# Mixer A of a two-layer backbone: GpSimd's subtraction reads the cumulated log-decays from the gates' tile, without VectorE's copy per head

## The chip, the cores and the metric

The kernel runs on one core of a Trainium2 chip. A core has five engines, each with its own queue of instructions, which it works off in order: TensorE (PE in the profile, with PEld for its weight loads), VectorE (DVE), ScalarE (ACT), GpSimd (POOL) and SyncE (SP), which here issues the transfers. They wait for one another through semaphores. The metric is the device time of one execution in microseconds, lower is better; for several runs the median is given.

## The reference

One inference step of a hybrid backbone with two layers, a width of 2048 and 640 tokens (128 context tokens, 512 latent tokens). The first layer has two mixers beside each other: gated-DeltaNet heads (mixer A) and windowed attention heads (mixer B). The second layer has gated linear attention and neighbourhood attention. Mixer A has 8 heads and works in chunks of 64 tokens, forwards and backwards. What matters here, for one head and one direction:

```python
gc = jnp.cumsum(g, -1)                                   # cumulated log-decays of a chunk
decay = jnp.exp(jnp.where(tri, gc[..., :, None] - gc[..., None, :], NEG))
lmat = jnp.where(strict, jnp.einsum('bhncd,bhnsd->bhncs', kb, k) * decay, 0.0)
attn = jnp.where(tri, jnp.einsum('bhncd,bhnsd->bhncs', q, k) * decay, 0.0)
```

The matrix of differences gc(c) - gc(s) is needed for each of the 10 chunks and the two directions; it enters both the triangular system `lmat`, which is then inverted, and the attention matrix `attn`.

## The kernel before

The weights are streamed from HBM in blocks of 128 x 512 (tile `w_st`). ScalarE rounds each block to a high part (`w_hi`, L1050) and VectorE subtracts this from the block for the low part (`w_lo`, L1052). TensorE multiplies the activations, split in the same way into `hh` and `hl`, in three products per block into PSUM tiles named `acc`. These products make up most of TensorE's work. All of them, and all small matmuls, go through one helper (L77).

Mixer A's heads run one after another through four stages, as generators: a convolution (`a_conv`), the preparation (`a_prep`), an inverse of the triangular matrices (`a_invert`, on GpSimd, with 60 small instructions and then one that transposes, L499), and the scan over the chunks (`a_scan`). Head h+1 is prepared while head h is inverted and scanned, and mixer B's heads and the weight products are laced in between. A planner in the kernel's own code chooses the order in which these generators issue: it keeps a clock that only matmuls advance and due times for each step. TensorE's order is fixed to that (`keep_in_program_order`). The orders of the other four queues are set by the framework, which sorts instructions by a simulated clock (`schedule_with_timeline_sim=True`) and puts in the semaphores. A tile with one buffer can only be written again when all readers of its former content are done; the framework makes the writer wait for that.

Before the heads, `a_gates` computes the gates of all heads once. The cumulated log-decays stand in the tile `g_gc` (128 partitions x 80 columns, ordered as direction o, chunk b, head h, so that one head's ten values lie 8 columns apart), and, transposed, in HBM (`gc_d`). `A["gc"]` is a view of `g_gc` with the axes o, b and h. In `a_prep`, for one head:

- SP issues two transfers that spread the head's rows of `gc_d` over 64 partitions each: tile `a_df`, 128 x 10 x 64, one buffer (L251).
- VectorE copies the head's ten columns of `g_gc` into `a_gcu`, 128 x 10, one buffer (L253).
- TensorE forms Gram matrices of the keys and the queries for their norms, VectorE reduces them (L270, L271), and a row of small VectorE instructions makes scale factors from them (L274 to L298).
- GpSimd subtracts `a_gcu`, each value repeated 64 times, from `a_df` in place (L301), and then adds a mask into `a_at` (L302).
- VectorE makes `a_M` from `a_df` (L309, L310), ScalarE takes exponentials, GpSimd scales `a_M` (L315).
- TensorE forms two more Gram products, each into a PSUM tile of the pool "gen", which has two buffers; VectorE multiplies them into `a_M` and `a_at` (L321), and the inverse starts with transfers of `a_M` to HBM and back into `i_S` (L482 to L489, GpSimd's first instruction is L491). Its results come back as `i_X` (L521), for the products `i_vps`.

The tiles of the pool "gen" are shared with the other small products, among them `ada_ps`, part of the modulation of later layers, which VectorE adds into `adv` (L1288). The scan's steps (L380 to L433) use PSUM tiles named `a_st`; VectorE's L410 and ScalarE's L412 both scale the same product, L427 updates the state. GpSimd's subtraction for head h+1 stands in GpSimd's queue right behind L315 of head h, ahead of the inverse of head h.

Of the kernel before, what the change touches and what calls it, by code (L numbers as in the profile page):

```python
# [8 lines left out]
F32 = mybir.dt.float32  # L9
# [3 lines left out]
ALU = mybir.AluOpType  # L13
# [76 lines left out]
def rsqrt(g, pool, x, n, tag, bufs=1):  # L90

    nc = g.nc
    y = pool.tile([128, n], F32, name=f"{tag}_y", tag=f"{tag}_y", bufs=bufs)[0:x.shape[0]]
    t = pool.tile([128, n], F32, name=f"{tag}_t", tag=f"{tag}_t")[0:x.shape[0]]
    yi = y.bitcast(I32)
    nc.vector.tensor_scalar(out=yi, in0=x.bitcast(I32), scalar1=1, scalar2=None, op0=ALU.logical_shift_right)
    nc.vector.tensor_scalar(out=yi, in0=yi, scalar1=-1.0, scalar2=float(0x5F3759DF), op0=ALU.mult, op1=ALU.add)
    for _ in range(3):
        nc.vector.tensor_mul(t, y, y)
        nc.vector.scalar_tensor_tensor(out=t, in0=t, scalar=-0.5, in1=x, op0=ALU.mult, op1=ALU.mult)  # L100
        nc.vector.scalar_tensor_tensor(out=y, in0=t, scalar=1.5, in1=y, op0=ALU.add, op1=ALU.mult)
    return y
# [137 lines left out]
def a_prep(g, h, qT, kT):  # L240

    nc, c, A = g.nc, g.c, g.A
    W, P1 = g.paw, g.pa1
    U = [128, 2, 5]
    hs = lambda t: t[:, :, :, h]
    bc = lambda t, n: t.unsqueeze(3).to_broadcast([128, 2, 5, n])


    df = W.tile([128, 10, 64], F32, name="a_df", bufs=1)
    for lo, hi in HALVES:  # L250
        nc.sync.dma_start(df[lo:hi], g.gcd[:, :, h, lo:hi].rearrange("o b s -> (o b) s").unsqueeze(0).to_broadcast([64, 10, 64]))  # L251
    gcu = W.tile([128, 10], F32, name="a_gcu")
    nc.vector.tensor_copy(gcu.rearrange("p (o b) -> p o b", o=2), hs(A["gc"]))  # L253
    b10 = lambda t: t.unsqueeze(2).to_broadcast([128, 10, 64])
    at = g.pe.tile([128, 2, 5, 64], F32, name="a_at", tag="a_at", bufs=2)
    M = P1.tile([128, 2, 5, 64], F32, name="a_M")
    def gram(x):

        ps = g.psg.tile([128, 5, 64], F32, name="a_gram", tag="gen")
        for b in range(5):  # L260
            for hf in range(2):
                cc = b * 128 + hf * 64
                g.mm(ps[hf * 64:hf * 64 + 64, b], lhsT=x[0][:, cc:cc + 64], rhs=x[1][:, cc:cc + 64], start=True, stop=True,
                     tile_position=(0, hf * 64))
        return ps

    ss = W.tile([128, 2, 5], F32, name="a_ss")
    for i, (x, sq) in enumerate(((kT, M), (qT, at))):
        ps = gram((x, x))
        nc.vector.tensor_tensor(out=sq[:, 0], in0=ps, in1=c["i64"].unsqueeze(1).to_broadcast([128, 5, 64]), op=ALU.mult)  # L270
        nc.vector.tensor_reduce(out=ss[:, i], in_=sq[:, 0], op=ALU.add, axis=mybir.AxisListType.X)  # L271
        yield
    sse = W.tile([128, 2, 5], F32, name="a_sse")
    nc.vector.tensor_scalar_add(sse, ss, 4 * EPS)  # L274
    rr = rsqrt(g, W, sse.rearrange("p a b -> p (a b)"), 10, "a_rr", bufs=2)
    rk, rq = rr[:, 0:5], rr[:, 5:10]
    rkb = rk.unsqueeze(1).to_broadcast(U)

    sm = lambda n: W.tile(U, F32, name=n, bufs=2)
    fm = c["fm"].rearrange("p (o b) -> p o b", o=2)  # L280
    bm = c["bm"].rearrange("p (o b) -> p o b", o=2)
    a = W.tile(U, F32, name="a_a")
    rk2 = W.tile([128, 5], F32, name="a_rk2")
    nc.vector.tensor_mul(rk2, rk, rk)
    nc.vector.tensor_mul(a, hs(A["beta"]), rk2.unsqueeze(1).to_broadcast(U))
    p2 = sm("a_p2")
    nc.vector.tensor_mul(p2, bm, sse[:, 0].unsqueeze(1).to_broadcast(U))
    nc.vector.tensor_add(p2, p2, hs(A["bfm"]))
    nc.vector.scalar_tensor_tensor(out=p2, in0=p2, scalar=0.5, in1=rkb, op0=ALU.mult, op1=ALU.mult)
    p1 = sm("a_p1")  # L290
    nc.vector.tensor_mul(p1, a, fm)
    nc.vector.tensor_add(p1, p1, bm)
    nc.vector.scalar_tensor_tensor(out=p1, in0=p1, scalar=-1.0, in1=hs(A["egc"]), op0=ALU.mult, op1=ALU.mult)
    c1 = sm("a_c1")
    nc.vector.tensor_mul(c1, a, bm)
    nc.vector.tensor_add(c1, c1, fm)
    c2 = sm("a_c2")
    nc.vector.tensor_mul(c2, c1, hs(A["dl"]))  # L298


    nc.gpsimd.tensor_tensor(out=df, in0=df, in1=b10(gcu), op=ALU.subtract)  # L301
    nc.gpsimd.tensor_tensor(out=at, in0=df.rearrange("p (o b) s -> p o b s", o=2),  # L302
                            in1=c["maskA"].rearrange("p (o s) -> p o s", o=2).unsqueeze(2).to_broadcast([128, 2, 5, 64]),
                            op=ALU.add)
    Mu = M.rearrange("p o b s -> p (o b) s")
    for o, (lo, hi) in enumerate(HALVES):
        f, b = slice(o * 5, o * 5 + 5), slice(5 - o * 5, 10 - o * 5)
        ms = c["maskS"][lo:hi].unsqueeze(1).to_broadcast([64, 5, 64])
        nc.vector.scalar_tensor_tensor(out=Mu[lo:hi, f], in0=df[lo:hi, f], scalar=-1.0, in1=ms, op0=ALU.mult, op1=ALU.add)  # L309
        nc.vector.tensor_tensor(out=Mu[lo:hi, b], in0=df[lo:hi, b], in1=ms, op=ALU.add)  # L310
    nc.scalar.activation(M, M, AF.Exp)
    nc.scalar.activation(at, at, AF.Exp)
    an = W.tile([128, 10], F32, name="a_an")
    nc.vector.tensor_scalar_mul(an, a.rearrange("p o b -> p (o b)"), -1.0)
    nc.gpsimd.tensor_tensor(out=Mu, in0=Mu, in1=b10(an), op=ALU.mult)  # L315


    yield LAT["gram"]
    for dst, x in ((M, kT), (at, qT)):
        ps = gram((kT, x))  # L320
        nc.vector.tensor_tensor(out=dst, in0=ps.unsqueeze(1).to_broadcast([128, 2, 5, 64]),  # L321
                                in1=dst, op=ALU.mult)
        if dst is M:
            inv = a_invert(g, M)
        yield
    return dict(h=h, qT=qT, kT=kT, inv=inv, at=at, p1=p1, p2=p2, c1=c1, c2=c2, rq=rq)
# [149 lines left out]
def a_invert(g, M):  # L476

    nc, W, P1 = g.nc, g.paw, g.pa1
    d1 = g.pd.tile([6, 10, 32, 32], F32, name="inv_in", tag="inv_in")
    for q in range(4):  # L480
        sub = q % 2
        nc.sync.dma_start(d1[q].rearrange("u i j -> i u j"),  # L482
                          M[q * 32:q * 32 + 32].rearrange("p o b s -> p (o b) s")[:, :, sub * 32:sub * 32 + 32])
        if sub == 1:
            nc.sync.dma_start(d1[4 + q // 2].rearrange("u i j -> i u j"),
                              M[q * 32:q * 32 + 32].rearrange("p o b s -> p (o b) s")[:, :, 0:32])
    SY = P1.tile([128, 1024], F32, name="i_S").rearrange("p (i j) -> p i j", i=32)
    S, Yt = SY[0:40], SY[64:104]
    nc.sync.dma_start(S, d1[0:4].rearrange("q u i j -> (q u) i j"))  # L489
    E = nc.gpsimd  # L490
    E.memset(S.rearrange("p i j -> p (i j)")[:, 0:1024:33], 1.0)  # L491
    for j in range(1, 31):
        n = 31 - j
        t = P1.tile([40, 240], F32, name="i_tmp", bufs=2)[:, 0:n * j].rearrange("p (a b) -> p a b", a=n)
        E.tensor_tensor(out=t, in0=S[:, j + 1:, j].unsqueeze(2).to_broadcast([40, n, j]),  # L495
                        in1=S[:, j, 0:j].unsqueeze(1).to_broadcast([40, n, j]), op=ALU.mult)
        E.tensor_tensor(out=S[:, j + 1:, 0:j], in0=S[:, j + 1:, 0:j], in1=t, op=ALU.add)  # L497
    Y = S
    E.tensor_tensor(out=Yt, in0=Y.rearrange("p i j -> p j i"), in1=g.c["ones"][0:40, 0:32].unsqueeze(1).to_broadcast([40, 32, 32]),  # L499
                    op=ALU.mult)  # L500
    d2 = g.pd.tile([2, 4, 10, 32, 32], F32, name="inv_out", tag="inv_out")
    nc.sync.dma_start(d2[0].rearrange("q u i j -> (q u) i j"), Y)
    nc.sync.dma_start(d2[1].rearrange("q u i j -> (q u) i j"), Yt)
    return d1, d2
# [1482 lines left out]
```

## Time and profile before

| | us |
|---|---|
| median of 3 runs | 2742.47 |
| lowest and highest | 2734.63 and 2742.68 |
| the profiled execution, its own time | 2739.52 |
| its span in the profile | 2737.7 |

The profile is of one execution. A row of a group or a timeline names line, engine, operation and tiles (written <- read); in a timeline the first number is the start in us from the span's start, the second the time it took, and in square brackets stands the idle time of the engine just before it with what ended it. In a table of waits stand the waiting instruction, whom it waited for, and the total in us, the number of times and the longest. The head's stage of mixer A lies between 180 and about 1110 us of the span. "Idle before" of an engine that is not the bottleneck costs nothing.

### The profile page before, as it was taken

The page shows a single profiled execution, that of the slowest core. Times are in us where ns is not written, and L with a number is a line of the kernel's source. Part 1 is how long each engine was busy: PE and PEld are TensorE (multiplying, and loading weights), DVE is VectorE, ACT ScalarE, POOL GpSimd, SP SyncE. Part 2 cuts the span into 40 slices and gives each one's busy share as a digit, 9 for nine tenths or more (in the row PEclk, how much of TensorE's full clock was granted, in tenths as well). Part 3 has the DMA queues.
Part 4 walks back from the last instruction along what each step waited for, and adds up shares of the span by engine and source line. Part 5 has one row for each costly group of instructions (what it writes and reads, how often), then busy time and mean ns, then how long its engine had stood idle before and what let it go on. Part 6 is the DMA issues. An engine that isn't in the chain of part 4 may idle for free. (4 is left out here: it accounts for less than half of the span.)

```text
span 2737.7 us, 54643 instructions
## 1 busy us (share of the span) xinstructions
PE 2606.5 (95%) x21303; PEld 2438.9 (89%) x21303; DVE 1542.8 (56%) x3606; ACT 954.4 (35%) x2150; POOL 703.9 (26%) x894
## 2 busy tenths in 40 slices
PE   6989999999999999999999899999999999999997
PEld 5778787988878897798999899999999999998996
DVE  5766546555556564447886745545553645545225
ACT  3232343423433343434224533343333334243222
POOL 2426604152342542001223330022001301221123
PEclk9989999999999999999999999999999999999998
DMA  9922333243333424236663423222232322325334
GB/s 336 314 88 83 115 94 107 87 120 107 91 116 100 137 68 121 82 110 221 193 203 119 129 70 105 95 86 86 88 115 80 95 88 90 101 68 182 94 101 135
DMA packets 264706, 329.85 MB, mean 120 GB/s; under 512 B 76013, under 2 KB 148925, under 8 KB 264447
## 3 DMA queue, kind: packets, MB, share of 16 engines
q1 hardware_dynamic: 264447, 326.35, 38.0%
q8 instruction: 168, 2.75, 0.4%
q14 instruction: 91, 0.75, 0.1%
HBM read 294.95 MB, written 28.68 MB: 118 GB/s over the span
## 5 line engine op out<-in xcount | busy, mean ns | idle before, releaser
L77 PE MATMUL acc<-hh,w_hi 128*128 128x320 f32 (+1 forms) x4544 | 1447.4, 320 | 15.7 <-ACT w_hi L1050 3.4
L77 PE MATMUL acc<-hl,w_hi 128*128 128x320 f32 (+1 forms) x4544 | 1416.1, 312 | 7.9 <-DVE hl L1230 7.7
L77 PE MATMUL acc<-hh,w_lo 128*128 128x320 f32 x4480 | 1394.0, 311 | 5.0 <-DVE w_lo L1052 5.0
L77 PEld LDWEIGHTS acc<-hh,w_hi 128*128 128x128 f32 (+1 forms) x4544 | 856.7, 189 | 56.7 <-issue 33.8
L77 PEld LDWEIGHTS acc<-hl,w_hi 128*128 128x128 f32 (+1 forms) x4544 | 857.5, 189 | 13.4 <-DVE hl L1230 11.5
L77 PEld LDWEIGHTS acc<-hh,w_lo 128*128 128x128 f32 x4480 | 846.8, 189 | 7.1 <-DVE w_lo L1052 6.3
L1052 DVE TENSOR_TENSOR w_lo<-w_st,w_hi 128x512 fp32r<-128x512 f32 x561 | 443.7, 792 | 583.3 <-ACT w_hi L1050 580.6
L1050 ACT CAST w_hi<-w_st 128x512 fp32r<-128x512 f32 (+1 forms) x604 | 365.0, 605 | 920.3 <-PE acc L77 790.9
L1321 DVE SCALAR_TENSOR_TENSOR vec<-vec,cond 128x256 f32<-128x256 f32 (+1 forms) x360 | 210.8, 629 | 24.0 <-DMA vec<-w_ada 22.3
L497 POOL TENSOR_TENSOR i_S<-i_S,i_tmp 40x30 f32<-40x30 f32 (+14 forms) x240 | 140.8, 587 | 18.7
L495 POOL TENSOR_TENSOR i_tmp<-i_S 40x30 f32<-40x30 f32 (+14 forms) x240 | 133.5, 556 | 18.0
L1464 POOL TENSOR_TENSOR n_acc<-n_acc,n_sq 128x640 f32<-128x640 f32 (+1 forms) x30 | 45.9, 1530 | 297.9 <-ACT n_sq L1463 297.9
L77 PE MATMUL ada_ps<-adv,cond 128*32 128x128 f32 x2048 | 93.6, 291 | 24.1 <-DMA adv<-w_ada 23.8
L930 POOL TENSOR_TENSOR c_X<-c_b 128x320 f32<-128x320 f32 x56 | 46.9, 838 | 221.5 <-PE c_lv L77 195.3
L77 PEld LDWEIGHTS ada_ps<-adv,cond 128*32 128x32 f32 x2048 | 48.0, 112 | 51.4 <-DVE n_acc L1464 19.9
L215 DVE SCALAR_TENSOR_TENSOR a_y<-a_pad,consts,a_y 128x644 f32<-128x644 f32 x96 | 92.1, 959 | 2.2
L791 POOL TENSOR_TENSOR d_bias<-d_braw,d_mask 128x256 f32<-128x256 f32 x32 | 29.1, 940 | 231.4 <-PE tm_ps L84 90.7
L1288 DVE TENSOR_TENSOR adv<-adv,ada_ps 128x128 f32<-128x128 f32 x144 | 40.5, 282 | 71.8 <-PE ada_ps L77 70.9
L302 POOL TENSOR_TENSOR a_at<-a_df,consts 128x640 f32<-128x640 f32 x8 | 13.6, 1695 | 258.1 <-DVE a_ss L271 226.2
L666 POOL TENSOR_TENSOR b_sw<-b_sw,b_tab 128x512 f32<-128x512 f32 x10 | 15.9, 1591 | 238.6 <-DMA b_sw<-b_q 221.8
L405 ACT ACTIVATE a_ot<-a_st,g_egc 128x128 f32<-128x128 f32 x72 | 26.4, 367 | 115.4 <-PE a_st L77 113.9
L616 ACT COPY at_P<-at_pt 128x384 f32<-128x384 f32 (+2 forms) x80 | 36.5, 456 | 76.4 <-PE at_pt L84 76.2
(311 smaller groups left out, 2768.5 us busy)
## 6 DMA issues: line engine op xcount, KB each, us to landing
adv<-w_ada SPq DMA_DIRECT2D x256, 256.0 KB
w_st<-w_in_odd SPq DMA_DIRECT2D x232, 256.0 KB
w_st<-w_in_even SPq DMA_DIRECT2D x188, 256.0 KB
w_st<-w_out_even SPq DMA_DIRECT2D x72, 256.0 KB
w_st<-w_out_odd SPq DMA_DIRECT2D x72, 256.0 KB
vec<-w_ada SPq DMA_DIRECT2D x64, 256.0 KB
vec<-w_ada SPq DMA_DIRECT2D x128, 128.0 KB
hl<-o_d SPq DMA_DIRECT2D x31, 320.0 KB
```

Of the source, the lines that this page charges most:

```text
L77: i = self.nc.tensor.matmul(out, lhsT=lhsT, rhs=rhs, **kw)
L215: nc.vector.scalar_tensor_tensor(out=y, in0=pad[:, j:j + CL], scalar=w[:, j:j + 1], in1=y, op0=ALU.mult, op1=ALU.add)
L495: E.tensor_tensor(out=t, in0=S[:, j + 1:, j].unsqueeze(2).to_broadcast([40, n, j]), in1=S[:, j, 0:j].unsqueeze(1).to_broadcast([40, n, j]) ...
L497: E.tensor_tensor(out=S[:, j + 1:, 0:j], in0=S[:, j + 1:, 0:j], in1=t, op=ALU.add)
L616: nc.scalar.copy(P[:, 0:nb], pt[:, 0:nb])
L791: nc.gpsimd.tensor_tensor(out=bias[:, j], in0=braw[:, :, x0:x0 + 32], in1=g.dmask[:, j * 32:j * 32 + 32].unsqueeze(1).to_broadcast([128, 8 ...
L930: nc.gpsimd.tensor_tensor(out=pv(X[0])[:, :, 1 - d], in0=bv[:, :, 1 - d], in1=bm, op=ALU.subtract)
L1050: nc.scalar.copy(hi, st)
L1052: (nc.gpsimd if g.spare >= 0 else nc.vector).tensor_tensor(out=lo, in0=st, in1=hi, op=ALU.subtract)
L1288: nc.vector.tensor_add(acc, acc, ps)
L1321: nc.vector.scalar_tensor_tensor(out=acc[:, c], in0=st, scalar=sc, in1=acc[:, c], op0=ALU.mult, op1=ALU.add)
L1464: eng.tensor_add(accs[0][:, cs], accs[0][:, cs], t[:, cs])
```

## The change

The copy into `a_gcu` and its tile are left out. GpSimd's subtraction reads the head's ten columns of `g_gc` itself, through the view with axes o and b, each value repeated 64 times; the tile `a_df` is viewed with the same axes. Nothing else is edited. `hs` picks a head's columns, `bc` adds the repeated axis; both were there.

```diff
     df = W.tile([128, 10, 64], F32, name="a_df", bufs=1)
     for lo, hi in HALVES:
         nc.sync.dma_start(df[lo:hi], g.gcd[:, :, h, lo:hi].rearrange("o b s -> (o b) s").unsqueeze(0).to_broadcast([64, 10, 64]))
-    gcu = W.tile([128, 10], F32, name="a_gcu")
-    nc.vector.tensor_copy(gcu.rearrange("p (o b) -> p o b", o=2), hs(A["gc"]))
     b10 = lambda t: t.unsqueeze(2).to_broadcast([128, 10, 64])
...
-    nc.gpsimd.tensor_tensor(out=df, in0=df, in1=b10(gcu), op=ALU.subtract)
+    d4 = df.rearrange("p (o b) s -> p o b s", o=2)
+    nc.gpsimd.tensor_tensor(out=d4, in0=d4, in1=bc(hs(A["gc"]), 64), op=ALU.subtract)
     nc.gpsimd.tensor_tensor(out=at, in0=df.rearrange("p (o b) s -> p o b s", o=2),
```

## The prediction

> **What bounds the kernel now.** I read the page first, then the table of waits by engine, then the timelines of TensorE (PE), VectorE (DVE) and GpSimd (POOL) around each copy that the change removes. The page's first part:
>
> ```profile
> span 2737.7 us, 54643 instructions
> PE 2606.5 (95%) x21303; PEld 2438.9 (89%) x21303; DVE 1542.8 (56%) x3606; ACT 954.4 (35%) x2150; POOL 703.9 (26%) x894
> ```
>
> PE is busy 95% of the span, so the kernel is as long as PE's work plus PE's gaps. What the change can win is a gap of PE, or a stretch in which PE's clock is low. The removed copy's own row, and the waits between 285 and 892 us, in which five of its eight runs fall:
>
> ```profile
> L253 DVE COPY a_gcu<-g_gc x8: 164/173/173, 184.2 to 783.5; 128x10 f32<-128x10 f32 x8
> ...
> DVE a_gcu L253 <- POOL a_df L301: 24.8, 5, 5.9
> ...
> PE a_gram L77 <- DVE adv L1288: 14.2, 4, 4.7
> PE a_st L77 <- ACT a_vno L412: 3.0, 6, 1.6
> ```
>
> The copy takes 0.17 us, but VectorE stands in front of it for 24.8 us in five runs. The tile a_gcu has one buffer. So the copy for head h+1 may not write it before GpSimd's subtraction for head h has read it, and that subtraction waits for the transfer of a_df. In the same time PE's second Gram product waits 14.2 us, in four cases, for VectorE's next instruction but a few (L1288). From the three engines' timelines the copy of head 2 (first row), and then the case of the copy of head 4:
>
> ```profile
> 209.68 0.17 DVE L253 COPY a_gcu<-g_gc 128x10 f32<-128x10 f32 x1 [1.73 <-POOL a_df L301]
> ...
> 437.55 0.17 DVE L253 COPY a_gcu<-g_gc 128x10 f32<-128x10 f32 x1 [5.46 <-POOL a_df L301]
> 438.36 0.28 DVE L1288 TENSOR_TENSOR adv<-adv,ada_ps 128x128 f32<-128x128 f32 x1
> ...
> 436.26 1.26 POOL L301 TENSOR_TENSOR a_df<-a_df,a_gcu 128x640 f32<-128x640 f32 x1 [5.46 <-DMA a_df<-gc_d]
> 447.52 0.15 POOL L491 MEMSET i_S<- 40x32 f32 x1 [10.00 <-DMA i_S<-inv_in]
> ...
> 433.15 0.80 PE L77 MATMUL a_gram<-a_o 128*64 128x64 f32 x20
> 438.70 1.33 PE L77 MATMUL a_gram<-a_o,a_o 128*64 128x64 f32 x20 [4.75 <-DVE adv L1288]
> 443.42 0.42 PE L77 MATMUL acc<-hh,w_hi 128*128 128x320 f32 x1
> ```
>
> The chain is: transfer of a_df, POOL's subtraction (to 437.52), the copy, three short VectorE instructions, L1288, which empties a PSUM buffer of the two in the pool "gen", and PE's second Gram product, which needs that buffer. PE idles 4.75 us and then runs slowly: twenty Gram matmuls take 1.33 us here, and 0.75 us where PE came without a gap (row 890.79 below). The granted clock in stretches of five us says the same:
>
> ```profile
> 439.00:444.00 5.00, 5.00 (x46) 3.92 (x43) 2.12 (x6) 0.81 (x2) 0.00 (x0) 0.57 0.34 52
> 292.00:297.00 5.00, 5.00 (x35) 4.01 (x34) 2.28 (x6) 0.71 (x3) 0.00 (x0) 0.66 0.44 86
> 889.00:894.00 5.00, 5.00 (x84) 3.69 (x84) 3.38 (x8) 1.98 (x5) 1.26 (x1) 1.00 0.81 240
> ```
>
> (PE's clock is the third number from the end.) The last row is the trace's own control: there head 6 is at the same place, head 7's subtraction runs on POOL as ever, but there is no copy for a ninth head. PE has no gap and the clock stays at 1.00.
>
> **The change part by part.** *Removed: eight copies on VectorE.* Their 8 x 0.17 = 1.4 us of busy time lie in an engine that is 56% busy; I take 0 for them. What counts is the wait that goes with them. I price each case by PE's timeline: from the last instruction before the gap to the first matmul at full clock again, against the same instructions in the control.
>
> ```profile
> 289.60 0.44 PE L77 MATMUL a_st<-a_r,a_Zt 64*64 64x128 f32 x4
> 291.59 0.44 PE L77 MATMUL a_st<-a_vno,a_at 64*64 64x128 f32 x4 [1.55 <-ACT a_vno L412]
> 296.75 0.42 PE L77 MATMUL acc<-hh,w_hi 128*128 128x320 f32 x1
> ...
> 545.96 0.80 PE L77 MATMUL a_gram<-a_o 128*64 128x64 f32 x20
> 560.05 0.42 PE L77 MATMUL acc<-hh,w_hi 128*128 128x320 f32 x1
> ...
> 658.34 0.80 PE L77 MATMUL a_gram<-a_o 128*64 128x64 f32 x20
> 668.58 0.31 PE L77 MATMUL acc<-hh,w_hi 128*128 128x320 f32 x1
> ...
> 780.94 0.80 PE L77 MATMUL a_gram<-a_o 128*64 128x64 f32 x20
> 784.32 1.12 PE L77 MATMUL a_gram<-a_o,a_o 128*64 128x64 f32 x20 [2.58 <-DVE adv L1288]
> 788.53 0.42 PE L77 MATMUL acc<-hh,w_hi 128*128 128x320 f32 x1
> ...
> 890.16 0.80 PE L77 MATMUL a_gram<-a_o 128*64 128x64 f32 x20
> 890.79 0.75 PE L77 MATMUL a_gram<-a_o,a_o 128*64 128x64 f32 x20
> 892.12 0.44 PE L77 MATMUL a_st<-a_r,a_Zt 64*64 64x128 f32 x4
> 893.12 0.43 PE L77 MATMUL ada_ps<-adv,cond 128*32 128x128 f32 x8
> 893.48 0.42 PE L77 MATMUL acc<-hh,w_hi 128*128 128x320 f32 x1
> 894.46 0.31 PE L77 MATMUL acc<-hh,w_hi 128*128 128x320 f32 x1
> 896.38 0.41 PE L77 MATMUL acc<-hh,w_hi 128*128 128x320 f32 x1
> ```
>
> In the control two Gram products, 3 acc matmuls, three groups of a_st and one ada_ps take 893.48 - 890.16 = 3.32 us (the three groups alone 893.12 - 892.12 = 1.00); 6 acc then take 0.98, and 12 acc, two groups of a_st and one ada_ps take 896.38 - 893.48 = 2.90.
> - Copy of head 7: 788.53 - 780.94 = 7.59 for work of 3.32; 4.27 is lost.
> - Head 6: 668.58 - 658.34 = 10.24 for 3.32 + 0.98 = 4.30; 5.94 lost.
> - Head 5: 560.05 - 545.96 = 14.09 for 3.32 + 2.90 = 6.22; 7.87 lost.
> - Head 4: 443.42 - 433.15 = 10.27 for two Gram products, 6 acc, two groups of a_st and an ada_ps: 3.32, less one group (0.33), plus three acc at 0.15 each, is 3.4; 6.9 lost. Here the instructions behind the copy were not ready when VectorE came to it: L427 needs a product that PE ends shortly before its first Gram product at 433.15, which I put at 432.9; and from the copy's start at 437.55 to L1288's end at 438.64 are 1.09 us. Without the copy L1288 ends near 433.95, and PE wants the buffer at 433.15 + 0.63 = 433.78. A gap of 0.3 stays: 6.6 won.
> - Head 3: 296.75 - 289.60 = 7.15 for 1.00 + 2.90 = 3.90; 3.25 lost. ScalarE's a_vno waited for VectorE's L410, which stood behind the copy.
> - Heads 0 to 2: VectorE waits 1.73 us at the copy of head 2, and PE has no gap there: 0.
>
> Together 4.27 + 5.94 + 7.87 + 6.6 + 3.25 = 27.9 us.
>
> On the clock the Trainium skill ("TensorE: Matmul & The Clock Gate", Part 1) says that the clock halves after an idle window of some 3.4 us. By that rule the gaps of 1.55 and 2.58 us would leave the clock alone, and with the one of head 6 only their idle time would be won: about 22 us in place of 27.9, a time near 2718. The trace does not agree: after 1.55 us of idle the granted clock fell to 0.66, and after 2.58 us the Gram matmuls took 1.12 instead of 0.75. I go by the trace.
>
> *Moved: the read of the log-decays.* POOL now takes one value of 10 per 64 columns from the tile g_gc, 8 values apart, with both operands in four dimensions. The trace has no such operation, so bounds:
>
> ```profile
> L499 POOL TENSOR_TENSOR i_S<-i_S,consts 40x1024 f32<-40x1024 f32 x8 | 24.7, 3089 | 0.6
> L302 POOL TENSOR_TENSOR a_at<-a_df,consts 128x640 f32<-128x640 f32 x8 | 13.6, 1695 | 258.1 <-DVE a_ss L271 226.2 <-PE ada_ps L77 31.8
> L315 POOL TENSOR_TENSOR a_M<-a_M,a_an 128x640 f32<-128x640 f32 x8 | 10.3, 1284 | 35.9 <-DVE a_p L292 35.9
> L301 POOL TENSOR_TENSOR a_df<-a_df,a_gcu 128x640 f32<-128x640 f32 x8 | 10.1, 1260 | 46.1 <-DMA a_df<-gc_d 41.0 <-DMA adv<-w_ada 5.1
> ```
>
> From below 1.26 us (nothing is left out of the operation, so no gain); from above L499, which reads a transposed operand at 3089/1024 = 3.0 ns per element, 1.93 us for 640. I take 1.28, L315's, since the 64-fold repeated value as inner dimension is what sets L301 and L315 apart from L302. What hides it: after the subtraction POOL waits for i_S, 10.00 us in the row at 447.52; the inverse cannot begin sooner. Uncovered is head 0 alone, where VectorE's L309 waits for the subtraction directly: 0 to 0.7 us there, and 0 is taken.
>
> The Trainium skill ("GPSIMD Engine Reference", section 7) speaks against this read: a step of more than 8 bytes costs half as much again per element. The step here is 32 bytes. By that rule the subtraction takes about 1.9 us and the sum loses 0.6 us in head 0; no run here has shown whether it holds where the inner step is zero.
>
> *Queues.* No transfer is added or moved. The transfers of a_df stand on SP's queue where they stood, since they wait for other readers of a_df. No wait is added either: POOL's subtraction waits for a_df's transfer as before, and g_gc is written once, before all heads. What comes next on VectorE and needs the subtraction is L309, after the next head's Gram products, tens of us on. Late next could be the inverse, which runs on POOL in its own time while PE gains on it by the slow stretches, at most 7.87 us in a head if all that is won there counts. Its last read is issued, and used by PE, at
>
> ```profile
> L521 SPq DMA_DIRECT2D i_X<-inv_out x4: 435/450/1458, 605.4 to 612.7; - x4
> ...
> 625.07 0.82 PE L77 MATMUL i_vps<-i_X,i_M 32*32 32x32 f32 x40
> ```
>
> which leaves 625.1 - 612.7 = 12 us less the landing. That holds.
>
> **The sum.** The profiled execution took 2739.52 us (2737.7 of span and 1.8 around it); 2739.52 - 27.9 = 2711.6. It lies 2.95 under the median of the runs, 2742.47; from the median it would be 2714.6. I say 2712.
>
> **Rivals.**
> 1. *The weights become the wait.* PE arrives 4 to 8 us earlier at matmuls whose weights pass through transfer, ScalarE and VectorE, and the gaps had given these time to catch up. Against it: PE had no wait for w_lo or w_hi between 285 and 892 us, and the control ran through with transfers at 240 GB/s. If half of each gap came back, 14 us are won: 2725.
> 2. *The time is absorbed, or the wait is still there.* The framework could hold VectorE at the same place for another reason, or PE's order could meet the inverse later (its 12 us against it). Then about 2739.
> 3. *Slower: the queues fall differently.* VectorE's, ScalarE's, POOL's and SP's orders come from the framework's simulated clock, and eight instructions less shift it. Place: a w_lo split (L1052) that comes to stand behind a VectorE instruction waiting for a slower engine, as the copy did. Price: a stall such as head 4's, 6.9 us. It decides from the fifth new stall on (27.9/6.9 = 4.0); six of them make 2711.6 + 41.4 = 2753. Against it: in the control VectorE's order is that of the other heads with the copy left out.
>
> **How the numbers follow.** Forecast 0.75, rival 1 0.12, rival 2 0.07, rival 3 0.06. The three runs shown spread over 8 us, 0.3%, which is about what can be told from no change. The forecast's own range is 2704 to 2720: 28.2 won at most (no gap left in head 4), 22 at least (0.7 lost in head 0, and a gap of up to 1 us left in each of the five places), and the spread of the runs. Reaching towards rivals 1 and 2 it becomes 2703 to 2732. Faster by over 0.3% (under 2734) holds the forecast and nearly all of rival 1: 0.85; within 0.3% 0.08; slower 0.07.
>
> **What would show it.** Right: L253 is gone; the wait of a_gram for L1288 falls from 14.2 us to under 1.5; the wait of a_st for a_vno falls from 3.0 to about 1.5; the clock is 1.00 in the stretches after the Gram products; the subtraction takes 1.26 to 1.93 us; i_vps never waits for i_X where it didn't; all of the gain lies between 285 and 892 us. Wrong: VectorE waits for the subtraction in another instruction; new waits of acc for w_lo; a gain under 15 us.

## The result, and the profile after

| | before | after |
|---|---|---|
| median, us | 2738.55 (4 runs) | 2719.69 (4 runs) |
| lowest and highest | 2734.34 to 2742.68 | 2718.48 to 2723.34 |
| ratio of the medians, 95% interval | | 0.9926 [0.9906, 0.9947] |
| the profiled execution, its own time | 2739.52 | 2723.34 |

The change wins 18.9 us, 0.7%; the interval says 14.5 to 25.7 (2738.55 x 0.0053 and x 0.0094). It is faster, as forecast, and the time lies in the range, but the forecast was a gain of 27.9 and a time of 2712. The question for the experiments is thus double: is the cause the one named, and where are the other 9 us?

The page's first part, of the changed kernel:

```profile
span 2721.5 us, 54637 instructions
...
PE 2601.2 (96%) x21303; PEld 2435.2 (89%) x21303; DVE 1536.9 (56%) x3598; ACT 954.0 (35%) x2150; POOL 704.9 (26%) x894
```

VectorE has eight instructions less, GpSimd and TensorE as many as before. Beyond the eight copies, the order of the instructions on VectorE, ScalarE, GpSimd and SyncE is the same in both traces, and TensorE's order is the same throughout.

TensorE's waits in the changed kernel between 285 and 892 us (waiting instruction, whom it waited for, total us, times, longest), the same stretch as in the prediction:

```profile
PE a_st L77 <- ACT a_vno L411: 5.0, 10, 1.1
PE a_st L77 <- DVE a_s L426: 3.4, 3, 1.5
PE at_s L77 <- DVE adv L1287: 1.7, 1, 1.7
```

The 14.2 us of a_gram's wait for VectorE's addition into adv have gone altogether. But a_st's wait for a_vno, which the prediction saw falling from 3.0 to about 1.5, stands at 5.0. This total says little about the change, since it differs as much between two traces of one kernel. Over the same stretch the second traces, taken later, of the kernel before (first row) and of the changed kernel have:

```profile
PE a_st L77 <- ACT a_vno L412: 5.2, 8, 1.6
...
PE a_st L77 <- ACT a_vno L411: 9.0, 11, 1.8
```

The forecast fall to 1.5 came in neither trace of the changed kernel.

Granted clock of the changed kernel in stretches of five us behind the places where TensorE stood before (stretch, length, busy time of PE, PEld, DVE, ACT and POOL with instruction counts, then the clock):

```profile
296.00:301.00 5.00, 5.00 (x48) 4.08 (x48) 2.21 (x6) 1.38 (x3) 0.45 (x1) 1.00 0.39 68
439.00:444.00 5.00, 4.93 (x50) 3.84 (x52) 2.72 (x6) 2.13 (x5) 1.28 (x1) 1.00 0.83 215
545.50:550.50 5.00, 5.00 (x67) 4.06 (x65) 4.11 (x9) 1.62 (x4) 1.28 (x1) 1.00 0.73 209
653.00:658.00 5.00, 5.00 (x54) 3.95 (x55) 2.46 (x8) 1.47 (x4) 0.61 (x1) 1.00 0.62 131
765.00:770.00 5.00, 4.97 (x84) 3.71 (x83) 3.40 (x7) 1.98 (x5) 1.28 (x1) 1.00 0.85 251
```

It is 1.00 in all five, where the kernel before had 0.57 and 0.66 in the stretches that the prediction shows. GpSimd's subtraction in the changed kernel, in the view of one tile's instructions (count, then shortest, median and longest ns, first and last start):

```profile
L300 POOL TENSOR_TENSOR a_df<-a_df,g_gc x8: 1277/1281/1283, 200.1 to 876.4; 128x640 f32<-128x640 f32 x8
```

1281 ns against 1260: the new read costs 0.02 us.

TensorE runs the same 21303 matmuls in the same order in every kernel of this study but the one with filled gaps, which has 360 more, so the time between the same two matmuls can be set side by side. This table is worked out from the starts of the matmuls in the traces, in us. A "place" is one of the five that the prediction priced, "behind" is the next 49 to 60 matmuls after four of them (that of head 3 has none). "Wait kept", "2 buf", "8 buf" and "rotary" are experiments below; a 2 marks a second trace of the same kernel.

```
                        before before2 wait kept  2 buf | after after2  8 buf rotary
start to gates' end     170.96  171.79   172.28  172.97 | 175.90 175.43 171.62 169.30
place of head 3           7.79    5.76     6.35    5.96 |   4.54   4.54   4.54   4.54
head 3 to head 4        136.25  142.60   138.20  137.65 | 137.12 145.36 137.30 141.38
place of head 4          10.33    9.85    10.31   10.21 |   3.88   4.25   3.76   4.27
place of head 5          13.88    9.99    13.70   10.79 |   6.00   6.02   6.02   6.02
place of head 6          10.75   10.53     9.72    9.43 |   4.82   4.82   4.82   4.82
place of head 7           7.25    8.06     9.86    3.68 |   2.98   3.21   2.98   2.98
the five places          50.00   44.19    49.94   40.07 |  22.22  22.84  22.12  22.63
four stretches behind    23.27   24.54    25.43   24.59 |  26.68  27.57  28.57  24.94
near 822 / 804 us         5.48    5.92     5.78    5.64 |   7.73   7.81   6.02   5.43
```

From the execution that the prediction read, the places fell by 50.00 - 22.22 = 27.8 us, against 27.9 forecast. What is missing lies in other rows: the places were worth less in the other execution of the kernel before, the stretches behind them became longer, and so did one stretch near 804 us. The start and the way from head 3 to head 4 vary by 7 and 9 us from one trace to the next with the same instructions, so one pair of profiled spans settles nothing here: 2737.7 - 2721.5 is 16.2. On the way from head 3 to head 4 the clock goes with it: it is at 0.50 for three stretches of 3.41 us in after2 (145.36), for two in before2 (142.60), for one each in the rotary kernel and in wait kept (141.38 and 138.20), and for none in the other four (136.25 to 137.65).

### The profile page after: what moved, and what is told of

The parts are those of the page before. It is cut to its first block, busy times and chain, and to the rows that moved or that the text cites. A ratio compares the mean times of both kernels' runs of the same rounds, so it can differ in the third digit from the quotient of the medians.

```text
span 2721.5 us, 54637 instructions
## 1 busy us (share of the span) xinstructions
PE 2601.2 (96%) x21303; PEld 2435.2 (89%) x21303; DVE 1536.9 (56%) x3598; ACT 954.0 (35%) x2150; POOL 704.9 (26%) x894
## 4 chain that ended last, share of the span: by engine, by line
PE 44%; DVE 3%; DMA 2%; issue 1%; ACT 0%; DVEq 0%; SPq 0%; ACTq 0%
PE acc L77 38%; PE at_s L77 1%; PE at_o L77 1%; DMA vec<-w_ada 1%; PE c_lv L77 1%; DVE hl L1774 1%; DVE vec L1320 1%; PE c_ops L77 1%; PE tm_ps L84 1%; PE c_U L77 0%; DVE x L1427 0%; PE at_pt L84 0%; DVE w_lo L1051 0%; PE c_bp L77 0%; DMA hl<-o_d 0%
## 5 line engine op out<-in xcount | busy, mean ns | idle before, releaser
L1320 DVE SCALAR_TENSOR_TENSOR vec<-vec,cond 128x256 f32<-128x256 f32 (+1 forms) x360 | 212.3, 634 | 23.3 <-DMA vec<-w_ada 21.5
L790 POOL TENSOR_TENSOR d_bias<-d_braw,d_mask 128x256 f32<-128x256 f32 x32 | 27.9, 905 | 231.8 <-PE tm_ps L84 90.7
L301 POOL TENSOR_TENSOR a_at<-a_df,consts 128x640 f32<-128x640 f32 x8 | 13.7, 1712 | 253.9 <-DVE a_ss L269 222.0
L665 POOL TENSOR_TENSOR b_sw<-b_sw,b_tab 128x512 f32<-128x512 f32 x10 | 14.9, 1491 | 234.8 <-DMA b_sw<-b_q 199.7
L1051 POOL TENSOR_TENSOR w_lo<-w_st,w_hi 128x256 fp32r<-128x256 f32 (+1 forms) x43 | 36.3, 851 | 106.6 <-ACT w_hi L1049 89.0
```

Source lines behind the costliest of these rows:

```text
L790: nc.gpsimd.tensor_tensor(out=bias[:, j], in0=braw[:, :, x0:x0 + 32], in1=g.dmask[:, j * 32:j * 32 + 32].unsqueeze(1).to_broadcast([128, 8 ...
L1051: (nc.gpsimd if g.spare >= 0 else nc.vector).tensor_tensor(out=lo, in0=st, in1=hi, op=ALU.subtract)
L1320: nc.vector.scalar_tensor_tensor(out=acc[:, c], in0=st, scalar=sc, in1=acc[:, c], op0=ALU.mult, op1=ALU.add)
```

## The experiments

**The changed kernel once more, and the kernel before once more.** No edit in either.

> The changed kernel once more, with more rounds. The first comparison gave a ratio of 0.9926 (0.9906 to 0.9947), 18.9 us between the medians, where 27.9 us were forecast. In its profiled execution the stretch before the gates was 4.5 us longer than in that of before, though the instructions there are the same, and the stretch from the gates to the end of the heads 23 us shorter. If the start only varies from run to run, the ratio comes out between 0.990 and 0.994 and the start of gc_ps in this profile lies anywhere between 179 and 185 us; if the change itself lengthens the start, gc_ps starts at 184 us again.

Measured: 2719.53 us (6 runs, 2713.23 to 2730.35) against 2737.85 (29 runs); ratio 0.9936 [0.9912, 0.9961], 17.5 us by the ratio. The five places took 22.84 us, and the stretch near 804 us 7.81. The gain and the two places where time was given back are thus the changed kernel's, not one execution's. The question of the start stays open: in this profile gc_ps begins at 184.0 us again, as the expectation put it for a change that lengthens the start, but in the rotary kernel below, which contains the change, it begins at 180.6.

> The kernel before, for a second profile. If the forecast's five prices are those of the kernel and not of one execution, the five places take 50 us in all again (7.79, 10.33, 13.88, 10.75 and 7.25), give or take 2 us each; the stretch up to 1733 matmuls (the end of the gates) took 171 to 176 us in five profiles of kernels that have the same instructions there, and comes out in the same range.

Measured: one run, 2749.18 us, too few to compare times; the five places took 44.19 us, not 50, so the forecast's prices were in part those of one execution. The place of head 5 took 9.99 us, 3.9 less than in the trace of the prediction. The two traces of the kernel before there, first the one that the prediction read, GpSimd's timeline and TensorE's:

```profile
548.59 1.26 POOL L301 TENSOR_TENSOR a_df<-a_df,a_gcu 128x640 f32<-128x640 f32 x1 [6.11 <-DMA a_df<-gc_d]
...
545.96 0.80 PE L77 MATMUL a_gram<-a_o 128*64 128x64 f32 x20
550.69 1.34 PE L77 MATMUL a_gram<-a_o,a_o 128*64 128x64 f32 x20 [3.93 <-DVE adv L1288]
```

and the second:

```profile
553.06 1.26 POOL L301 TENSOR_TENSOR a_df<-a_df,a_gcu 128x640 f32<-128x640 f32 x1 [4.68 <-DMA a_df<-gc_d]
...
552.08 0.80 PE L77 MATMUL a_gram<-a_o 128*64 128x64 f32 x20
555.17 1.10 PE L77 MATMUL a_gram<-a_o,a_o 128*64 128x64 f32 x20 [2.29 <-DVE adv L1288]
```

In the first GpSimd's subtraction begins 2.6 us after TensorE's first Gram product, in the second 1.0. TensorE's gap shrinks by the same 1.6 us, and the low clock behind it lasts 3.41 us in place of 10.24 (first trace, then second; the clock is the third number from the end):

```profile
549.10:559.34 10.24, 8.65 (x59) 6.93 (x61) 5.55 (x14) 1.67 (x4) 0.74 (x1) 0.50 0.42 110
...
555.49:558.90 3.41, 3.41 (x33) 2.58 (x27) 2.13 (x3) 1.59 (x4) 0.00 (x0) 0.50 0.31 48
```

What the wait costs hangs on when the transfer of a_df lands beside TensorE's progress, and this differs between executions.

**The wait put back, the strided read kept.** The changed kernel, with the copy into the one-buffered a_gcu as before, and a small new GpSimd instruction that reads it behind the subtraction (an extra tile of 128 x 10 that nothing uses; nothing is left out):

```diff
-    nc.gpsimd.tensor_tensor(out=df, in0=df, in1=b10(gcu), op=ALU.subtract)
+    d4 = df.rearrange("p (o b) s -> p o b s", o=2)
+    nc.gpsimd.tensor_tensor(out=d4, in0=d4, in1=bc(hs(A["gc"]), 64), op=ALU.subtract)
+    late = W.tile([128, 10], F32, name="a_late")
+    nc.gpsimd.tensor_tensor(out=late, in0=gcu, in1=df[:, :, 0], op=ALU.add)
```

> The changed kernel with the wait put back: VectorE again copies the head's log-decays into a one-buffer tile, but the subtraction reads the gates' tile as in the change, and a small GpSimd instruction behind it (128x10) is the copy's only reader. If the wait is the cause, this gives the time of before or a little more (ratio 0.998 to 1.002), with VectorE idle some 25 us in front of the copy and PE's a_gram waiting some 14 us. If it is the strided read or the copy's absence that wins, it stays near 0.993. The extra instruction's result is used by nothing.

Measured: 2742.90 us (12 runs), ratio 1.0017 [1.0004, 1.0031]. The waits between 180 and 1000 us (VectorE) and between 180 and 1150 us (TensorE):

```profile
DVE a_gcu L253 <- POOL a_late L304: 28.4, 6, 6.8
...
PE a_gram L77 <- DVE adv L1291: 15.4, 4, 4.9
```

The new read alone wins nothing. With the wait back, VectorE's stall, TensorE's gaps and the five places (49.94 us) are back as well.

**Eight buffers for a_gcu.** The kernel before; copies and contiguous read stay, only the reason for the wait goes:

```diff
-    gcu = W.tile([128, 10], F32, name="a_gcu")
+    gcu = W.tile([128, 10], F32, name="a_gcu", bufs=8)
```

> Two buffers left the wait (VectorE 21.5 us in front of five copies, PE's a_gram 10.6 us in three places in place of 14.2 in four): the framework issues each copy as soon as a buffer comes free, so a second buffer only moves every copy one head ahead, to the same places, and one of the five went, that ahead of 784 us. With eight buffers no copy has a former reader. If the wait is the whole cause, all eight copies run without idle time before them, the five places take in all 22 us as in the changed kernel (50 us before), and the time is that of the changed kernel (ratio 0.991 to 0.996) although all copies are there and GpSimd reads the copy. If the two buffers gave little because the copy itself or the read is the cause, it stays near 0.998.

Measured: 2716.43 us (6 runs) against 2739.10 (11 runs), ratio 0.9917 [0.9903, 0.9932]. The copies in this kernel (count, shortest, median and longest ns, first and last start):

```profile
L253 DVE COPY a_gcu<-g_gc x8: 153/165/168, 184.5 to 185.3; 128x10 f32<-128x10 f32 x8
```

All eight run within a microsecond, before the heads. a_gcu is not among VectorE's waits any more, and the five places take 22.12 us. With the run before this closes the case from both sides: the wait makes the whole difference, the copies' own work and the form of GpSimd's read make none that can be measured.

**Two buffers for a_gcu.** The kernel before with `bufs=2` on that line instead.

> The kernel before with two buffers for a_gcu and nothing else: the eight copies stay, GpSimd reads the copy as before, but the copy of a head no longer waits for the subtraction of the head ahead of it. If that wait is the cause, the time is that of the changed kernel (ratio to before 0.990 to 0.994), the copies take 0.17 us each without idle time before them, and PE's 14.2 us of waits of a_gram for L1288 are gone. If the copy's work or GpSimd's read of a small contiguous tile is the cause, it stays at 1.000.

Measured: 2734.22 us (12 runs), ratio 0.9982 [0.9965, 0.9998], far from what was expected. The copies, in the same view:

```profile
L253 DVE COPY a_gcu<-g_gc x8: 154/172/174, 186.0 to 658.4; 128x10 f32<-128x10 f32 x8
```

and the waits between 180 and 1000 us (VectorE) and 180 and 1150 us (TensorE):

```profile
DVE a_gcu L253 <- POOL a_df L301: 21.5, 5, 5.3
...
PE a_gram L77 <- DVE adv L1288: 10.6, 3, 4.6
```

The last copy starts at 658.4 us instead of 783.5. Each copy moved one head forward, to the place where a buffer comes free, and there it stands behind the same subtraction on the same transfer. Only the place of head 7, for which no copy was left, went: 3.68 us against 7.25 to 9.86. The two-buffer expectation assumed that the copy would stay where it was; that the framework queues it as soon as its simulated clock has a buffer free is read from these starts.

**TensorE's gaps filled with work.** The kernel before; the first of the two later Gram products is issued again 6, 5, 4 and 3 times in heads 2 to 5 (at the places of the copies of heads 4 to 7), with the same values into the same tile. These 360 matmuls are extra; the planner's clock does not count them.

```diff
+        for _ in range(again):
+            for b in range(5):
+                for hf in range(2):
+                    cc = b * 128 + hf * 64
+                    g.tc.keep_in_program_order(nc.tensor.matmul(
+                        ps[hf * 64:hf * 64 + 64, b], lhsT=x[0][:, cc:cc + 64], rhs=x[1][:, cc:cc + 64], start=True,
+                        stop=True, tile_position=(0, hf * 64)))
...
-        ps = gram((kT, x))
+        ps = gram((kT, x), {2: 6, 3: 5, 4: 4, 5: 3}.get(h, 0) if dst is M else 0)
```

> The kernel before, with the wait as it was, but TensorE repeats the first Gram product 6, 5, 4 and 3 times more in heads 2 to 5 (each repeat some 0.63 us), where it would idle 4.75, 3.93, 2.94 and 2.58 us; the last pass overwrites the others, so the result is the same. The wait ends at the same time, so the idle time itself is not won. If the slow stretches after the gaps come from the idle time, they shrink or go: 2.15 + 3.94 + 3.0 + 1.69 = 10.8 us at most, a ratio down to 0.996. If the clock falls at this place for another reason, or the pauses that are left (under 1 us) are enough, the ratio stays at 1.000.

Measured: 2731.56 us (11 runs), ratio 0.9974 [0.996, 0.9989]: 7.1 us less, with 360 matmuls more. VectorE's wait between 180 and 1000 us, TensorE's between 285 and 900 us, and the clock behind the four places:

```profile
DVE a_gcu L253 <- POOL a_df L308: 24.3, 6, 5.4
...
PE a_gram L77 <- DVE adv L1295: 2.1, 3, 1.0
```

```profile
441.50:446.50 5.00, 5.00 (x62) 4.08 (x58) 2.86 (x7) 2.13 (x5) 0.00 (x0) 1.00 0.34 53
550.60:555.60 5.00, 5.00 (x54) 3.89 (x53) 2.89 (x8) 1.25 (x3) 0.00 (x0) 1.00 0.35 53
660.00:665.00 5.00, 5.00 (x63) 4.06 (x63) 3.61 (x9) 1.61 (x4) 0.00 (x0) 1.00 0.36 58
777.50:782.50 5.00, 5.00 (x63) 4.06 (x63) 3.57 (x9) 1.62 (x4) 0.00 (x0) 1.00 0.36 57
```

VectorE still stands in front of the copies (24.3 us here, 26.5 in the kernel before over the same stretch), but TensorE is busy meanwhile, keeps its clock at 1.00, and the kernel gains by it. So the low clock behind a gap is a cost by itself. By the prediction's prices the clock's share in these four places is 24.7 - 13.9 = 10.8 us (their sum less the idle time, the 0.3 us of head 4 left out); 7.1 were measured, with 3.0 to 10.9 as its interval. By the starts of the matmuls (the added ones left out) the four places took 29.6 us here, against 41.4 over the three traces with the wait.

**The rotary product moved to VectorE.** The changed kernel; near 804 us TensorE waits for VectorE, and VectorE for a product of GpSimd (L665), which stands behind the inverse's instructions. The timelines of the changed kernel there (VectorE, GpSimd, TensorE):

```profile
802.15 1.10 DVE L667 TENSOR_TENSOR b_q<-b_q,b_sw 128x512 f32<-128x512 f32 x1 [1.73 <-POOL b_sw L665]
...
800.84 1.28 POOL L665 TENSOR_TENSOR b_sw<-b_sw,b_tab 128x512 f32<-128x512 f32 x1
...
804.54 0.58 PE L77 MATMUL a_st<-a_s,a_wT 128*64 128x128 f32 x3 [1.52 <-DVE a_s L426]
```

and the stretch behind it, with the clock as the third number from the end:

```profile
804.00:810.00 6.00, 5.46 (x41) 4.16 (x41) 1.93 (x8) 1.65 (x5) 5.29 (x10) 0.72 0.28 87
```

The edit takes that hand-over away:

```diff
-    nc.gpsimd.tensor_tensor(out=sw, in0=sw, in1=g.sin, op=ALU.mult)
+    nc.vector.tensor_tensor(out=sw, in0=sw, in1=g.sin, op=ALU.mult)
```

> The changed kernel, and in mixer B's rotary step the product with the sine table moves from GpSimd to VectorE (10 products of 128x512). In the changed kernel PE lost 2.25 us near 804 us against before: VectorE's L667 waits there 1.73 us for GpSimd's product, which stands behind an instruction of the inverse, and the state update behind it comes late for PE (1.52 us of idle, and then a clock of 0.72). If that is what gave back part of the gain, the stretch around 804 us shrinks from 7.7 to at most 5.5 us, and the time falls 2 to 4 us below the changed kernel's (ratio 0.991 to 0.993). If VectorE's ten products of some 0.7 us are in the way elsewhere, or the wait for the transfer b_sw comes in place of GpSimd's, it stays at 0.994 or rises.

Measured: 2717.53 us (6 runs), ratio to the kernel before 0.9926 [0.991, 0.9943]. TensorE's longest wait for a_s in this kernel, between 180 and 1150 us:

```profile
PE a_st L77 <- DVE a_s L426: 1.4, 3, 0.7
```

The stretch near 804 us falls from 7.73 to 5.43 us, back to where it stood before the change. That 2 us are lost there through this hand-over is thus shown in the trace; in the time of the whole kernel it can't be told from the changed kernel's. Nor must it come with the change: with eight buffers, where VectorE is freed too, TensorE's gap there was 1.31 us in place of 1.52, the clock stayed at 1.00, and the stretch took 6.02 us. No kernel here is clearly better than the changed one: the one with eight buffers lies within its interval too.

## Why the prediction was right, and where its sum was off

- *The cause* (one buffer of a_gcu, VectorE held by GpSimd's subtraction, TensorE's second Gram product behind VectorE). Right, shown from both sides: the wait alone put back gives the old time (ratio 1.0017), the wait alone taken away gives 0.9917.
- *The prices of the places.* By the trace that the prediction read, and by that of the changed kernel: head 7, 4.27 forecast and 7.25 - 2.98 = 4.27 measured; head 6, 5.94 and 5.93; head 5, 7.87 and 7.88; head 4, 6.6 and 6.45 (the gap of 0.3 us that was to stay did not show; the place took 0.5 us more than the control's price all the same; the working's own difference, 433.95 less 433.78, is 0.17); head 3, 3.25 and 3.25. The control (the same instructions a head later, where no copy stood) was a sound measure of what is left without the wait. What the places cost with the wait is another matter: by the second traces of both kernels the same places fell by 44.19 - 22.84 = 21.4 us, so that 27.8 met 27.9 so closely is owed to the one trace that was priced.
- *The low clock behind the gaps.* Right that it costs: 1.00 in all five places of the changed kernel, and a gain by filling the gaps alone. Its size at head 3 was chance: there the clock was low in the trace of the prediction (the place took 7.79 us), but not in the three other traces that have this stall (5.76 to 6.35). The Trainium skill ("TensorE: Matmul & The Clock Gate", Part 1) has an idle window of some 3.4 us as what halves the clock. As a rule on single gaps, the way the prediction put it against its own price, these runs do not bear it out: behind 1.52 us of idle the changed kernel has 0.72, above, and the places of heads 6 and 7, with gaps of 2.94 and 2.58 us, fell by 5.93 and 4.27, more than those gaps. The 2718 us that the prediction worked out from it lie nearer to the measured 2719.69 than its own 2712, but not for that reason.
- *The new read.* Right: 1.28 us, and the trace does not show the surcharge of half as much again that the Trainium skill ("GPSIMD Engine Reference", section 7) has for a step of more than 8 bytes; the 32-byte step is not the innermost one here. That the repeated inner value is what makes L301 and L315 quicker than L302, as the prediction has it, was not tried; these two also write in place, and L302 does not.
- *Queues, the inverse and the weights.* Right: no order changed, so rival 3 fell; i_vps does not wait for i_X between 285 and 892 us, and acc has no wait for w_lo or w_hi among TensorE's rows, so rival 1 did not come as described. Rival 2 fell with the cause.
- *The sum.* This is the step that failed: "Together 4.27 + 5.94 + 7.87 + 6.6 + 3.25 = 27.9 us", taken as the kernel's gain. Three things were missing. First, it priced one execution as if it were the middle. Over the three traces with the wait (before, before2, wait kept) the places take 48.0 us, over the two of the changed kernel 22.5: 25.5, not 27.8. Second, each price ended at the first matmul at full clock, so what came right behind was left out. The four stretches behind grew from 24.4 (the three) to 27.1 us (the two), 2.7 us back. In both traces of the changed kernel, and with eight buffers, each of these stretches has one gap, of 0.43 to 1.51 us, in front of a product of the scan (a_st); in the three traces with the wait none has one above 0.15 us. With two buffers only the stretch behind head 7 has one, the place where the wait had gone. That the full clock alone brings these gaps is not so: with the filled gaps, at 1.00, the four stretches took 23.3 us. Nor do they always come: the rotary kernel has them in two of the four, 24.94 us in all. The control had such a gap as well, 3.3 us behind the point where my working stopped. The control in the kernel before, and the same step of two heads in the changed kernel:

```profile
899.69 0.44 PE L77 MATMUL a_st<-a_vno,a_at 64*64 64x128 f32 x4 [0.93 <-ACT a_vno L412]
```

```profile
775.49 0.44 PE L77 MATMUL a_st<-a_vno,a_at 64*64 64x128 f32 x4 [0.73 <-ACT a_vno L411]
...
884.00 0.44 PE L77 MATMUL a_st<-a_vno,a_at 64*64 64x128 f32 x4 [1.11 <-ACT a_vno L411]
```

Third, TensorE's gain on GpSimd was checked against the inverse alone; the rotary product that waits behind the inverse on the same queue gave 7.8 - 5.7 = 2.0 us back near 804 us, most of it through the low clock (the gap itself took 1.52 and 1.60 us, against 0.77 to 1.21 with the wait). Together 25.5 - 2.7 - 2.0 = 20.8, against 18.9 and 17.5 measured. This account is rough: the same working gives 21.5 us for eight buffers, 25.2 for the rotary kernel and 14.0 for the filled gaps, where 22.7, 20.3 and 7.1 were measured. It also leaves out the start, which took 175.9 and 175.4 us in the two traces against 171.0 to 172.3 in the three. So the traces show that the five places cost less in another execution and that some time comes back at the next hand-overs; how the missing 9 us divide stays open.

## What to carry to other kernels

A tile with one buffer can hold up a whole engine: where an instruction of 0.17 us has idle time before it that ends at another engine's read of the same tile, look at what stands behind it in the queue, and at the slowed matmuls behind each gap of TensorE. Before adding a buffer, ask where the writer will then be put: two buffers only moved this copy one head ahead into the same stall, while one per head, or no tile at all, took the stall away (three to seven were not tried). A price taken between two points of one timeline should run on past the next hand-over, and from more than one execution, before it is called the gain.

## What the runs showed of the hardware

- TensorE's granted clock was either 1.00 or 0.50 in these traces, and it changed at points that lie whole multiples of 3.41 us apart (in the kernel before, for example, from 293.10 to 549.10 us, 256.00 or 75 times 3.413). In the changed kernel the clock fell 1.6 us after the end of the gap of 1.52 us (at 804.54), while behind 1.11 us (884.00) it stayed at 1.00. One row of the kernel before, then two of the changed one:

```profile
293.10:296.51 3.41, 3.41 (x21) 2.75 (x24) 0.70 (x5) 0.05 (x1) 0.00 (x0) 0.50 0.52 84
...
806.12:809.53 3.41, 3.41 (x16) 2.78 (x14) 0.25 (x2) 0.68 (x2) 3.02 (x6) 0.50 0.27 89
...
884.00:890.00 6.00, 6.00 (x58) 4.75 (x58) 2.15 (x7) 1.55 (x5) 4.90 (x13) 1.00 0.66 196
```

With the wait put back, a gap of 1.59 us left the clock alone and one of 1.20 us, a little later, did not:

```profile
292.01 0.44 PE L77 MATMUL a_st<-a_vno,a_at 64*64 64x128 f32 x4 [1.59 <-ACT a_vno L415]
299.28 0.44 PE L77 MATMUL a_st<-a_vno,a_at 64*64 64x128 f32 x4 [1.20 <-ACT a_vno L415]
...
290.59:294.00 3.41, 1.99 (x16) 1.70 (x17) 2.87 (x8) 1.18 (x3) 0.43 (x2) 1.00 0.08 14
294.00:297.42 3.42, 3.42 (x34) 2.86 (x32) 0.70 (x3) 0.37 (x1) 0.00 (x0) 1.00 0.58 110
300.83:304.25 3.42, 3.42 (x18) 3.09 (x18) 0.54 (x3) 0.41 (x2) 2.76 (x9) 0.50 0.57 190
```

In the kernel before even 2.67 us of idle, divided between two such stretches, left it at 1.00:

```profile
714.07 1.16 PE L77 MATMUL at_o<-at_P,b_v 128*128 128x128 f32 x8 [2.67 <-ACT at_P L616]
...
709.53:712.94 3.41, 1.87 (x14) 1.60 (x12) 3.30 (x6) 0.96 (x4) 2.33 (x1) 1.00 0.31 107
712.94:716.35 3.41, 2.29 (x18) 2.29 (x19) 0.87 (x3) 2.60 (x9) 0.00 (x0) 1.00 0.44 93
```

No length of gap that decides comes out of these traces.

- A single VectorE instruction can take several times its usual time, for no reason that the trace shows. In the second trace of the changed kernel (in the first, the 40 runs of this line took 273 to 634 ns):

```profile
339.86 2.77 DVE L406 TENSOR_TENSOR a_ot<-a_oraw,a_ot 128x128 f32<-128x128 f32 x1
```

In that trace the way from head 3 to head 4 took 145.36 us instead of 137.12. The clock was low three times on it, as said under the table; what part this one instruction has was not tried.
